# Attention's output projection and the final projection in blocks of seven products, at the head of the feed-forward's sequence

## The chip, the core and the metric

One core of a Trainium2 chip runs the whole kernel. The metric is device time in microseconds (us). TensorE (PE) multiplies matrices out of SBUF into PSUM, VectorE (DVE) and ScalarE (ACT) work on elements, GpSimd (POOL) does a few small things, and SyncE (SP) issues nearly all DMAs. Each engine works off its own list of instructions in order; semaphores make one wait for another.

## The reference, cut to what matters

A block of an encoder on 256 tokens of width 2048: a retention branch and a latent attention branch, merged by gates, then a feed-forward of width 8192. The stretch that the change is about:

```python
def _mixer(...):
    ...
    y_mla = my.reshape(B, S, MLA_V_W) @ w_mla_o                 # 256x2048 @ 2048x2048
    merged = jax.nn.sigmoid(g_ret) * y_ret + jax.nn.sigmoid(g_mla) * y_mla
    return merged @ w_out                                        # 256x2048 @ 2048x2048

def reference(...):
    ...
        h = h + _mixer(...)
        z = _rmsnorm(h, norm_mlp_g[l]) @ w_up[l]                 # 2048x8192
        h = h + jnp.square(jax.nn.relu(z)) @ w_down[l]           # 8192x2048
    return _rmsnorm(h, norm_f_g)
```

All inputs are float32.

## The kernel before, in words

**Products of two halves.** Every float32 operand is split into a rounded part `hi` and the remainder `lo`; a product is three matmuls (hi x hi, hi x lo, lo x hi). For weights the split is one cast on ACT (`hi`) and one subtraction on DVE (`lo`) of a tile of 128x1024, in `weights` (lines L168 and L169) or in `split` (L550 and L551). `hi` and `lo` lie in rings of buffers (4, in some stages 7), the raw weights in a ring of five.

**Eight and seven products.** Most large products are cut into blocks: two 128-row pieces of the inner dimension, two halves of the tokens (t), two column pieces of 512 (c). Done plainly (`Eight`), a block is eight products, 24 matmuls, in two parts of one weight tile each. Done by a Strassen-like scheme (`Seven`), it is seven products, 21 matmuls, in four parts. `Seven` needs sums of weights (`forms`, three DVE operations, L307, L316 and L317), splits of three 128x1024 tiles and one 128x512 tile, and sums of tokens (`combine`, L231 to L241 and a split), which one set serves for all columns. Its results pile up in four additional PSUM banks, and `partial` turns these into four corrections (`rest`) at the end of a half, a half being 1024 columns. The table `SEVEN` says at which places of the eight blocks of a half the sevens stand.

**What sets the order.** In the stages written with parts, `stream` lays out the order by hand (`manual_schedule`): at step n it issues the loads up to part n+6, the splits (`prep`) up to part n+4, the matmuls of part n, then what `after(n)` and the list `later` (steps to wait, work) hold for this step. Elsewhere a scheduler orders instructions.

**Around the change.** The attention's output projection (`mo`, `w_mla_o`) and the final projection (`wo`, `w_out`) are plain: `n_unit` walks over four column quarters of 512, each with two PSUM tiles (one per token half) and 16 inner pieces; L214, L215 and L217 are its three matmuls. Both are 384 matmuls. The first quarters of `mo` are interleaved with the last four attention heads. As a quarter of `mo` ends, `merge` multiplies it by its gate `gm` and adds `m1`, `merge_turn` transposes the result and splits it into `mg`, the final projection's tokens. As a quarter of `wo` ends, DVE adds it to the residual `hn` (L1220) and ACT sums its squares (L1221); `mlp_turn` transposes `hn` and cuts it into `hT` (L553, L554), the feed-forward's tokens, and `hc.make` forms their combinations. Then the feed-forward's `stream` begins with three early units (`z`), each in two halves, the first halves first; the second halves need all of `hT`. Steps of seven products (`zs`) and further units follow, and last the down projection (`dn`), of whose 64 blocks 22 are sevens.

Of the kernel before, what the change touches and what calls it, by code (L numbers as in the profile page):

```python
# [12 lines left out]
F32 = mybir.dt.float32  # L13
F32R = mybir.dt.float32r
# [5 lines left out]
P = 128  # L20
S = 256
# [20 lines left out]
KP = KT // 2  # L42
XC = 2, 10
EARLIES = 7, 15, 60
SEVEN = {"rv": ((2, 4, 5), (2, 4, 5)), "gr": ((3, 5), (2, 4, 5)), "yr": ((2, 4, 5), (2, 4, 5)), "gm": ((3, 5, 6), (2, 4, 5))}
DS = (4, 7, 9, 12, 14, 17, 19, 22, 24, 27), (3, 5, 7, 9, 11, 13, 15, 17, 19, 21, 24, 27)
KEPT = 3
MORE = 3
# [57 lines left out]
def block_kernel(ctx: ExitStack, tc: tile.TileContext, A):  # L106
# [233 lines left out]

    class Banks:
        def __init__(self, name, half, pairs, steps):
            self.name, self.half, self.q = name, half, {}
# [15 lines left out]
            PE.matmul(q, al, wh, start=False, stop=self.left[f] == 0)  # L359

    class Tokens:
        def __init__(self, pair, j, sets):
            self.pair, self.j, self.sets = pair, j, sets

        def load(self):
            pass
# [7 lines left out]
        def get(self, f):  # L374
            if f in Combos.RAW:
                return self.block(*Combos.RAW[f])
            c = self.sets[:, self.j]
            return c[:, 0, Combos.FORM[f]], c[:, 1, Combos.FORM[f]]

    class Eight:  # L380
# [528 lines left out]
    with ExitStack() as mctx:  # L909
# [159 lines left out]

        cq, ckv = Lora(cc[:, :LT]), Lora(cc[:, LT:])  # L1070
        mg = Pair("mg")
        mo = {}

        def mla_projections(g):
            j0 = 2 * (g % 2)
# [44 lines left out]
            SC.copy(v1, pss[1])  # L1120
            heads[g, "v"] = vs, v1

        def mo_part(c, kp):
            src = A["w_mla_o"][4 * c + kp // 2][:, kp % 2 * 2 : kp % 2 * 2 + 2]
            n_unit(mo[c], src, my, 2 * kp, 2, kp == 0, kp == 7)

        def mla_out_begin():
            for c in range(2):
                mo[c] = [mmps(f"mo{c}{t}") for t in range(2)]
            for kps in (range(4), range(4, 6)):  # L1130
                for c in range(2):
                    for kp in kps:
                        mo_part(c, kp)
                        yield

        SLOTS = (
            ((0, 2, 4, 6), (4, 6, 8, 10), (6, 8, 10, 12)),
# [23 lines left out]
        def merge(c):  # L1161
            cs = slice(c * 512, (c + 1) * 512)
            for t, ps in enumerate(mo[c]):
                V.tensor_tensor(out=gm[:, t, cs], in0=ps, in1=gm[:, t, cs], op=ALU.mult)
                V.tensor_tensor(out=gm[:, t, cs], in0=gm[:, t, cs], in1=m1[:, t, cs], op=ALU.add)

        def merge_turn(c):
            for jj in range(2):
                pT = atps(f"mt{c}{jj}")
                for j in range(2):  # L1170
                    for t in range(2):
                        o = j * S + t * P
                        k = 4 * c + 2 * jj + j
                        PE.transpose(pT[:, o : o + P], gm[:, t, k * P : (k + 1) * P], ident)
                split(*mg.span(4 * c + 2 * jj, 2), pT.rearrange("p (j n) -> p j n", j=2))

        for c in range(2):
            for kp in (6, 7):
                mo_part(c, kp)
            merge(c)  # L1180
        for c in range(2, 4):
            mo[c] = n_cols("mo", A["w_mla_o"], my, c, [None, lambda: merge_turn(c - 2), lambda: merge_turn(c - 1)][: c])
            merge(c)
        for c in (2, 3):
            merge_turn(c)

    rctx.close()
    hn = big("hn", shape=(P, 2, D))
    nc.sync.dma_start(hn, A["x"].rearrange("(t p) d -> p t d", p=P))
    hT = Pair("hT")  # L1190

    def mlp_turn(c):
        for jj in range(2):
            pT = atps(f"ht{c}{jj}")
            for j in range(2):
                kt = 4 * c + 2 * jj + j
                for t in range(2):
                    o = j * S + t * P
                    PE.transpose(pT[:, o : o + P], hn[:, t, kt * P : (kt + 1) * P], ident)
            for j in range(2):  # L1200
                kt = 4 * c + 2 * jj + j
                g = vec[:, V_MLP + kt : V_MLP + kt + 1]
                split(hT.hi(kt), hT.lo(kt), pT[:, j * S : (j + 1) * S], scale=g)
    zp = ctx.enter_context(tc.tile_pool(name="zp", bufs=1))
    hidd = ctx.enter_context(tc.tile_pool(name="hidd", bufs=1, space=bass.MemoryType.DRAM))
    hc = Combos("hc", hT)
    ssh = cp.tile([P, 2, 4], F32, name="ssh")
    rh2 = cp.tile([P, 2], F32, name="rh2")
    for c in range(4):
        cs = slice(c * 512, (c + 1) * 512)  # L1210
        pss = [mmps(f"wo{c}{t}") for t in range(2)]
        for kq in range(4):
            n_unit(pss, A["w_out"][4 * c + kq], mg, 4 * kq, 4, kq == 0, kq == 3)
            if kq == 0 and c:
                mlp_turn(c - 1)
        if c in (1, 2):
            for _ in hc.make(c - 1):
                pass
        for t in range(2):
            V.tensor_tensor(out=hn[:, t, cs], in0=pss[t], in1=hn[:, t, cs], op=ALU.add)  # L1220
            SC.activation(pss[t], hn[:, t, cs], AF.Square, accum_out=ssh[:, t, c : c + 1])  # L1221
    for t in range(2):
        V.reduce_sum(rh2[:, t : t + 1], ssh[:, t], axis=mybir.AxisListType.X)
    V.tensor_scalar(rh2, rh2, 1.0 / D, EPS, op0=ALU.mult, op1=ALU.add)
    V.reciprocal(rh2, rh2)

    hid = [hidd.tile([P, 2, S], F32, name=f"hid{i}") for i in range(FT // 2)]
    forms = big("forms", shape=(P, 4, 2, 512))

    def store(pair, n, t):  # L1230
        SC.activation(t, t, AF.Square)
# [7 lines left out]
    class Unit:  # L1239
# [11 lines left out]

        def mm(self, part):
            if part == 0:
                self.ps = atps(f"z{self.i}")
# [49 lines left out]
        return fn  # L1304

    early = [Unit(i, 0) for i in range(EARLY)]
    parts = [(e, h) for h in range(2) for e in early]
    units = list(range(EARLY, FT - ST - LATE))
    slots = [(u, j, h) for u in range(SU) for j in range(SJ) for h in (1, 3)][:-1]
    whole = [t for t in slots if t[2] == 3]  # L1310
# [17 lines left out]
        un = Unit(i, 0, drain(((0, 1), (1, 2))[n]))  # L1328
        parts += [(un, 0), (un, 1)]

    hp = ctx.enter_context(tc.tile_pool(name="hp", bufs=1))
    combs, sets = {}, {}
    ssf = cp.tile([P, 2, SSF], F32, name="ssf")
    rf = cp.tile([P, 2], F32, name="rf")
# [124 lines left out]
    making = iter(())  # L1459

    def after(n):
        nonlocal making, zo, keep, hn2, gt
        if n == 0:
            mlp_turn(3)
# [3 lines left out]
        elif n in MAKE:  # L1468
            making = hc.make(2 + MAKE.index(n))
        if n < 2 * EARLY or n % 2 == 0:  # L1470
            next(making, None)
        if hooks.get(n) == 0:
            hn2 = big("hn2", shape=(P, 2, D))
            G.dma_start(hn2, keep)
            gt = big("gt", shape=(P, 2, D))
            G.dma_start(gt[:, 0], A["norm_f_g"].partition_broadcast(P))
        elif hooks.get(n) == 1:
            for t in range(2):
                for c in range(2):
                    def one(t=t, c=c):  # L1480
                        later.append([1, finish(0, t, c, c)])

                    later.append([2 * t + c, one])
                    later.append([6 + 2 * t + c, lambda t=t, c=c: scale(t, c)])

    zo = keep = hn2 = gt = None
    rings(zp, MORE, True, forms)
    with tc.manual_schedule(engines=MANUAL):
        stream(parts, after)
        assert not later  # L1490
# [100 lines left out]
```

## Time and profile before

| | |
|---|---|
| median of 3 runs | 1566.04 us (1565.64 to 1566.29) |
| the profiled execution | 1566.54 us, of which 1564.8 from the first to the last instruction |
| busy: PE, DVE, ACT | 1551.3, 1316.0, 962.6 us |
| matmuls of `mo`, first and last start | 685.3 and 786.4 us |
| matmuls of `wo`, first and last start | 787.4 and 877.9 us |
| first matmul of the early units, of `zs` | 878.2 and 895.8 us |

A row of a timeline is start, duration, engine, line, operation, output <- inputs by the program's names, the shape, and in brackets the idle time of the engine before it and what ended that. A row of groups ends with busy time and mean duration in ns, then the engine's idle time before these instructions. A row of a stretch gives its length, the busy time of PE, weight loads, DVE, ACT and POOL, the granted TensorE clock (1.00 is full), the DMA's share and GB/s. Matmuls are drawn longer than the distance between their starts, since they overlap.

### The profile page before, as it was taken

The numbers are of one execution on the slowest core, as the hardware profiler recorded it, in microseconds if no ns is written. First come the engines' busy times: TensorE is split into PE (matmuls) and PEld (weight loads), VectorE is DVE, ScalarE is ACT, GpSimd is POOL, SyncE is SP. The second block draws the span as 40 slices with busy tenths as digits, with TensorE's granted clock in tenths as the row PEclk, the third lists the DMA queues.
The fourth block names the chain that finished last, engine by engine and source line by source line (L and its number), as shares of the span: only waits on it lengthen the run. The fifth ranks groups of instructions, "written<-read, shape, count | busy, mean of one in ns | idle before, by whom it ended". The sixth has DMA issues, their size and how long they took to land.

```text
span 1564.8 us, 21391 instructions
## 1 busy us (share of the span) xinstructions
PE 1551.3 (99%) x7655; PEld 1311.0 (84%) x7655; DVE 1316.0 (84%) x1787; ACT 962.6 (62%) x1416; POOL 39.3 (3%) x76
## 2 busy tenths in 40 slices
PE   9999999999999999999999999999999999999997
PEld 7888888888898888888888888888888888888886
DVE  7898877799976988976567689887978899989996
ACT  6645655566545667875445567676767766656664
POOL 0000000000000000000000000000000100000000
PEclk9999999999999999999999999999999999999999
DMA  9666755566656654444556657666675977686873
GB/s 319 207 203 208 230 164 161 159 201 206 206 168 220 213 197 143 157 136 161 185 206 211 236 196 247 214 226 232 207 249 188 376 265 245 237 304 211 266 255 115
DMA packets 107626, 333.70 MB, mean 213 GB/s; under 512 B 11264, under 2 KB 12160, under 8 KB 106496
## 3 DMA queue, kind: packets, MB, share of 16 engines
q1 hardware_dynamic: 104208, 318.71, 61.1%
q0 software_dynamic: 3168, 11.54, 1.9%
q10 hardware_dynamic: 144, 2.10, 0.4%
q8 instruction: 60, 0.98, 0.3%
q14 instruction: 46, 0.38, 0.1%
HBM read 319.72 MB, written 12.58 MB: 212 GB/s over the span
## 4 chain that ended last, share of the span: by engine, by line
PE 79%; DVE 1%; issue 1%; ACT 1%; DVEq 0%; POOLq 0%; POOL 0%; ACTq 0%
PE z L176 9%; PE dn L358 7%; PE dn L359 7%; PE dn L357 7%; PE z L180 5%; PE zs L333 2%; PE zs L334 2%; PE zs L335 2%; PE mo L214 2%; PE mo L215 2%; PE mo L217 2%; PE wo L214 2%; PE wo L215 2%; PE wo L217 2%; PE gm L357 2%; PE yr L358 2%
## 5 line engine op out<-in xcount | busy, mean ns | idle before, releaser
L551 DVE TENSOR_TENSOR lo<-raw,hi 128x1024 fp32r<-128x1024 f32 (+3 forms) x214 | 232.0, 1101 | 22.7 <-ACT hi L550 22.2
L169 DVE TENSOR_TENSOR lo<-raw,hi 128x1024 fp32r<-128x1024 f32 (+1 forms) x148 | 173.2, 1171 | 89.7 <-ACT hi L168 89.6
L168 ACT CAST hi<-raw 128x1024 fp32r<-128x1024 f32 (+1 forms) x148 | 149.6, 1011 | 155.9 <-PE mo L215 44.9
L550 ACT CAST hi<-raw 128x1024 fp32r<-128x1024 f32 (+3 forms) x214 | 200.0, 953 | 55.3 <-issue 9.5
L551 DVE TENSOR_TENSOR morelo<-raw,morehi 128x1024 fp32r<-128x1024 f32 (+1 forms) x118 | 127.1, 1098 | 18.8 <-ACT morehi L550 18.3
L550 ACT CAST morehi<-raw 128x1024 fp32r<-128x1024 f32 (+1 forms) x118 | 109.1, 949 | 10.5 <-issue 3.2
L550 ACT CAST hi<-forms 128x1024 fp32r<-128x1024 f32 x70 | 73.7, 1052 | 51.2 <-DVE forms L307 28.1
L176 PE MATMUL z<-hT,morehi 128*128 128x512 f32 x408 | 101.6, 391 | 0.0
L357 PE MATMUL dn<-hi,dd 128*128 128x512 f32 x230 | 89.6, 389 | 0.0
L359 PE MATMUL dn<-hi,dd 128*128 128x512 f32 x230 | 89.5, 389 | 0.0
L358 PE MATMUL dn<-lo,dd 128*128 128x512 f32 x230 | 89.5, 389 | 0.0
L551 DVE TENSOR_TENSOR lo<-forms,hi 128x1024 fp32r<-128x1024 f32 x70 | 85.0, 1221 | 5.3 <-ACT hi L550 4.9
L176 PEld LDWEIGHTS z<-hT,morehi 128*128 128x128 f32 x408 | 74.9, 188 | 14.4
L1266 ACT COPY hs<-z 128x512 f32<-128x512 f32 x40 | 23.5, 587 | 71.2 <-PE z L180 71.1
L357 PE MATMUL dn<-morehi,dd 128*128 128x512 f32 x156 | 60.7, 389 | 0.0
L358 PE MATMUL dn<-morelo,dd 128*128 128x512 f32 x156 | 60.7, 389 | 0.0
L359 PE MATMUL dn<-morehi,dd 128*128 128x512 f32 x156 | 60.7, 389 | 0.0
L180 PEld LDWEIGHTS z<-hT,morelo 128*128 128x128 f32 x408 | 55.6, 190 | 4.0
L176 PE MATMUL z<-hT,hi 128*128 128x512 f32 x232 | 57.9, 392 | 0.0
L180 PE MATMUL z<-hT,morelo 128*128 128x256 f32 x408 | 56.9, 282 | 0.0
L307 DVE TENSOR_TENSOR forms<-raw,sraw 128x1024 f32<-128x1024 f32 x46 | 56.1, 1219 | 0.3 <-DMA raw<-w_up_s 0.3
L358 PEld LDWEIGHTS dn<-lo,dd 128*128 128x128 f32 x230 | 43.2, 188 | 9.0
(500 smaller groups left out, 4193.9 us busy)
## 6 DMA issues: line engine op xcount, KB each, us to landing
raw<-w_down SPq DMA_DIRECT2D x106, 512.0 KB, 6.0
raw<-w_up SPq DMA_DIRECT2D x80, 512.0 KB, 5.1
raw<-w_rv SPq DMA_DIRECT2D x32, 512.0 KB, 4.8
raw<-w_rg SPq DMA_DIRECT2D x32, 512.0 KB, 4.3
raw<-w_gret SPq DMA_DIRECT2D x32, 512.0 KB, 4.4
raw<-w_ret_o SPq DMA_DIRECT2D x32, 512.0 KB, 5.0
raw<-w_gmla SPq DMA_DIRECT2D x32, 512.0 KB, 4.3
raw<-w_mla_o SPq DMA_DIRECT2D x32, 512.0 KB, 3.7
```

Of the source, the lines that this page charges most:

```text
L168: SC.copy(hi, raw)
L169: V.tensor_tensor(out=lo, in0=raw, in1=hi.bitcast(F32), op=ALU.subtract)
L176: PE.matmul(out, w[0][:, k], x.both(k0 + k), start=start and k == 0, stop=False)
L180: PE.matmul(out[:, :S], w[1][:, k], x.hi(k0 + k), start=False, stop=stop and k == n - 1)
L214: PE.matmul(out, x.hi(k0 + k, ts), w[0][:, k], start=start and k == 0, stop=False)
L215: PE.matmul(out, x.lo(k0 + k, ts), w[0][:, k], start=False, stop=False)
L217: PE.matmul(out, x.hi(k0 + k, ts), w[1][:, k], start=False, stop=stop and k == nk - 1)
L357: PE.matmul(q, ah, wh, start=start, stop=False)
L358: PE.matmul(q, ah, wl, start=False, stop=False)
L359: PE.matmul(q, al, wh, start=False, stop=self.left[f] == 0)
L550: SC.copy(hi, val)
L551: V.tensor_tensor(out=lo, in0=val, in1=hi.bitcast(F32), op=ALU.subtract)
```

## The change

Both projections are taken out of the scheduled part and become 68 parts of blocks at the head of the feed-forward's `stream` (the first six blocks of `mo`'s first half stay interleaved with the attention). `mo`'s second half has three sevens (blocks 0, 1, 2), `wo`'s first half two (4, 5) and its second three (4, 5, 6): eight of 32 blocks. The weights are laid out on the host in the order of the blocks. `merged`, `summed` and `begun` (the correction's addition ahead of the last block) take the place of the loops' ends; `plan` holds what happens after which part: transposes, combinations of tokens, the load of the residual. The early units become four, and the last transposes of `hn` follow the first three of their halves.

```diff
-EARLY, LATE = 3, 2
+EARLY, LATE = 4, 2
...
-MAKE = 7, 2 * EARLY + 18
+MAKE = 9, 2 * EARLY + 18
...
-SEVEN = {... "gm": ((3, 5, 6), (2, 4, 5))}
+SEVEN = {... "gm": ((3, 5, 6), (2, 4, 5)), "mo": ((), (4, 5, 6)), "wo": ((5, 6), (4, 5, 6))}
...
-        for c in range(2, 4):
-            mo[c] = n_cols("mo", A["w_mla_o"], my, c, [None, lambda: merge_turn(c - 2), lambda: merge_turn(c - 1)][: c])
-            merge(c)
-        for c in (2, 3):
-            merge_turn(c)
...
-    for c in range(4):
-        cs = slice(c * 512, (c + 1) * 512)
-        pss = [mmps(f"wo{c}{t}") for t in range(2)]
-        for kq in range(4):
-            n_unit(pss, A["w_out"][4 * c + kq], mg, 4 * kq, 4, kq == 0, kq == 3)
-            if kq == 0 and c:
-                mlp_turn(c - 1)
-        if c in (1, 2):
-            for _ in hc.make(c - 1):
-                pass
...
+    def merged(banks, t, c):
+        ...
+        if banks.rest:
+            r = banks.rest[t, c]
+            V.tensor_tensor(out=r, in0=p, in1=r, op=ALU.add)
+            p = r
+        V.tensor_tensor(out=g, in0=p, in1=g, op=ALU.mult)
+        V.tensor_tensor(out=g, in0=g, in1=m1[:, t, cs], op=ALU.add)
+
+    def summed(banks, t, c):
+        n = 2 * banks.half + c
+        h = hn[:, t, n * 512 : (n + 1) * 512]
+        V.tensor_tensor(out=h, in0=banks.q[ROLE[t, c]], in1=h, op=ALU.add)
+        SC.activation(banks.rest[t, c], h, AF.Square, accum_out=ssh[:, t, n : n + 1])
+
+    def begun(banks, t, c):
+        o = (2 * banks.half + c) * 512
+        h = hn[:, t, o : o + 512]
+        V.tensor_tensor(out=h, in0=banks.rest[t, c], in1=h, op=ALU.add)
+
+    def half_of(banks, src, x, seq, sets, first, done, soonest, early=None):
+        ...
+        def end():
+            sums = partial(banks, wsums)
+            later.extend([d, lambda: next(sums)] for d in range(2))
+            if early:
+                later.extend([1 + (t == 0), lambda t=t, c=c: early(banks, t, c)] for t in (1, 0) for c in range(2))
+
+        def over(part):
+            if part:
+                for c in range(2):
+                    for t in range(2):
+                        later.append([soonest[t, c], lambda t=t, c=c: done(banks, t, c)])
+        ...
+    slow = {(0, 0): 0, (1, 0): 1, (0, 1): 2, (1, 1): 3}
+    fast = {(0, 0): 0, (1, 0): 0, (0, 1): 1, (1, 1): 1}
+    half_of(mob[0], A["w_mla_o"], my, E8(6, 7), None, 0, merged, slow)
+    at(0, lambda: make(my, 0, wsets[0][:, :2]))
+    at(3, lambda: make(my, 2, wsets[0][:, 2:]))
+    base = len(parts)
+    half_of(mob[1], A["w_mla_o"], my, E8(3, 4, 5, 6) + S7(0, 1, 2) + E8(7), wsets[0], 0, merged, slow)
+    for i in range(4):
+        at(base + 3 + i, lambda i=i: merge_turn(i // 2, i % 2, mmps))
+    ...
+    half_of(wob[0], A["w_out"], mg, E8(0, 1, 2, 3, 7) + S7(4, 5) + E8(6), wsets[1], 4, summed, slow, begun)
+    at(base + 1, lambda: nc.sync.dma_start(hn, A["x"].rearrange("(t p) d -> p t d", p=P)))
+    for i in range(4):
+        at(base + 3 + i, lambda i=i: merge_turn(2 + i // 2, i % 2, atps))
+    at(base + 6, lambda: make(mg, 4, wsets[1][:, :2]))
+    at(base + 11, lambda: make(mg, 6, wsets[1][:, 2:]))
+    base = len(parts)
+    half_of(wob[1], A["w_out"], mg, E8(0, 1, 2, 3) + S7(4, 5, 6) + E8(7), wsets[1], 4, summed, fast, begun)
+    ...
+    for i in range(4):
+        at(base + 3 + i, lambda i=i: turned(i // 2, i % 2, mmps, 1))
+    at(base + 8, lambda: makings.append(hc.make(0)))
+    at(base + 14, lambda: makings.append(hc.make(1)))
+    off = len(parts)
+    for n, i in enumerate((0, 1, 2, 2)):
+        at(off + i, lambda n=n: turned(2 + n // 2, n % 2, atps, 0))
```

How the order moves, at three places. The first is ScalarE where a piece of the final projection is added to the residual: `hi` are casts of weights, the ACTIVATE with `ssh` is the sum of squares of `hn`. Before, at the end of the first quarter:

```order
L168 CAST hi_7606<-raw_7605 128x1024
L168 CAST hi_7624<-raw_7623 128x1024
L1221 ACTIVATE wo_7399,ssh<-hn 128x512
L1221 ACTIVATE wo_7400,ssh<-hn 128x512
L168 CAST hi_7642<-raw_7641 128x1024
L168 CAST hi_7660<-raw_7659 128x1024
```

Now, at the end of the first half:

```order
L550 CAST hi_7834<-raw_7797 128x1024
L1218 ACTIVATE wsums,ssh<-hn 128x512
L550 CAST hi_7856<-raw_7810 128x1024
L1218 ACTIVATE wsums,ssh<-hn 128x512
L550 CAST hi_7880<-raw_7832 128x1024
L1218 ACTIVATE wsums,ssh<-hn 128x512
```

The squares stood in pairs, and now stand singly, each ahead of one cast. The second place is VectorE at the same ends, where `lo` is the split that follows the cast `hi` of the same row. Before, at the end of the second quarter:

```order
L169 TENSOR_TENSOR lo_7785<-raw_7783,hi_7784 128x1024
L1220 TENSOR_TENSOR hn<-wo_7549,hn 128x512
L1220 TENSOR_TENSOR hn<-wo_7550,hn 128x512
L169 TENSOR_TENSOR lo_7803<-raw_7801,hi_7802 128x1024
L169 TENSOR_TENSOR lo_7821<-raw_7819,hi_7820 128x1024
```

Now, at the end of the first half, behind the additions of the corrections (`wsums`):

```order
L1223 TENSOR_TENSOR hn<-wsums,hn 128x512 x2
L551 TENSOR_TENSOR lo_7835<-raw_7797,hi_7834 128x1024
L1223 TENSOR_TENSOR hn<-wsums,hn 128x512 x2
L1217 TENSOR_TENSOR hn<-wo_7480,hn 128x512
L551 TENSOR_TENSOR lo_7857<-raw_7810,hi_7856 128x1024
L1217 TENSOR_TENSOR hn<-wo_7488,hn 128x512
L551 TENSOR_TENSOR lo_7881<-raw_7832,hi_7880 128x1024
```

Four additions alternate with four splits, where two stood together, and four more additions stand ahead. The third place is TensorE at the step from the final projection to the feed-forward; `ht` are transposes of `hn`. Before:

```order
L217 MATMUL wo_7905<-lo_8052,mg_5247 128x512 x2
L176 MATMUL z_8138<-hT_7390,hi_8126 128x512 x8
L180 MATMUL z_8138<-hT_7390,lo_8127 128x256 x8
L1199 MATMUL ht_8155<-con,hn 128x128 x4
L1199 MATMUL ht_8164<-con,hn 128x128 x4
L176 MATMUL z_8194<-hT_7390,hi_8130 128x512 x8
```

Now:

```order
L359 MATMUL wo_7872<-morehi_67_8166,mg_5247 128x512
L176 MATMUL z_8260<-hT_6939,morehi_68_8180 128x512 x8
L180 MATMUL z_8260<-hT_6939,morelo_68_8181 128x256 x8
L1169 MATMUL ht_8277<-con,hn 128x128 x4
L176 MATMUL z_8296<-hT_6939,morehi_69_8192 128x512 x8
L180 MATMUL z_8296<-hT_6939,morelo_69_8193 128x256 x8
L1169 MATMUL ht_8313<-con,hn 128x128 x4
```

The transposes behind the first early half are now those of the third quarter of `hn`, and the fourth quarter's come two halves later.

More of the change, by code (lines that the diff above doesn't have):

```diff
@@ L361, in block_kernel, with __init__ @@
     class Tokens:
-        def __init__(self, pair, j, sets):
-            self.pair, self.j, self.sets = pair, j, sets
+        def __init__(self, pair, j, sets, first=0):
+            self.pair, self.j, self.sets, self.first = pair, j, sets, first
         def load(self):
@@ L1121, in mla_projections @@
             heads[g, "v"] = vs, v1
-        def mo_part(c, kp):
-            src = A["w_mla_o"][4 * c + kp // 2][:, kp % 2 * 2 : kp % 2 * 2 + 2]
-            n_unit(mo[c], src, my, 2 * kp, 2, kp == 0, kp == 7)
+        mob = [Banks("mo", half, KP, len(at)) for half, at in enumerate(SEVEN["mo"])]
         def mla_out_begin():
[L1128 to L1134, printed above, removed]
+            rings(None, 0, False, None)
+            for j in range(6):
+                d = Eight(mob[0], A["w_mla_o"][0, j], Tokens(my, j, None))
+                for part in range(2):
+                    d.load(part)
+                    d.prep(part)
+                    d.mm(part)
+                    yield
         SLOTS = (
@@ new lines, in summed @@
+    def summed(banks, t, c):
[4 more added lines that the diff above has]
+    def begun(banks, t, c):
+        o = (2 * banks.half + c) * 512
+        h = hn[:, t, o : o + 512]
+        V.tensor_tensor(out=h, in0=banks.rest[t, c], in1=h, op=ALU.add)
+    steps = 0
+    def half_of(banks, src, x, seq, sets, first, done, soonest, early=None):
+        nonlocal steps
+        last = max((m for m, (k, j) in enumerate(seq) if k == 7), default=None)
+        def end():
[6 more added lines that the diff above has]
+                for c in range(2):
+                    for t in range(2):
+                        later.append([soonest[t, c], lambda t=t, c=c: done(banks, t, c)])
+        for m, (k, j) in enumerate(seq):
+            if k == 7:
+                st = Seven(banks, src[banks.half, j], Tokens(x, j, sets, first), steps, end if m == last else None)
+                parts.extend((st, h) for h in range(4))
+                steps += 1
+            else:
+                st = Eight(banks, src[banks.half, j], Tokens(x, j, None))
+                parts.extend((st, h) for h in range(2))
+        st.after = over
@@ L1306, in block_kernel @@
     early = [Unit(i, 0) for i in range(EARLY)]
-    parts = [(e, h) for h in range(2) for e in early]
+    parts += [(e, h) for h in range(2) for e in early]
     units = list(range(EARLY, FT - ST - LATE))
```

112 lines of the change are left out of this document (60 added, 52 removed).

## The prediction

> **What bounds the kernel now.** I read the page's busy times first, then the stretches in which the two projections run, then the groups inside one of them.
>
> ```profile
> PE 1551.3 (99%) x7655; PEld 1311.0 (84%) x7655; DVE 1316.0 (84%) x1787; ACT 962.6 (62%) x1416; POOL 39.3 (3%) x76
> ...
> 729.50:787.40 57.90, 57.90 (x274) 48.28 (x272) 36.84 (x41) 24.83 (x28) 0.00 (x0) 1.00 0.61 203
> 787.40:878.20 90.80, 90.80 (x420) 75.46 (x418) 59.10 (x69) 45.17 (x62) 0.00 (x0) 1.00 0.60 200
> 878.20:895.80 17.60, 17.60 (x106) 15.59 (x105) 13.31 (x21) 11.07 (x17) 0.00 (x0) 1.00 0.72 263
> 1300.00:1400.00 100.00, 100.00 (x443) 82.81 (x442) 96.71 (x121) 62.60 (x80) 0.00 (x0) 1.00 0.76 265
> ...
> L169 DVE TENSOR_TENSOR lo<-raw,hi 128x1024 fp32r<-128x1024 f32 x29 | 35.5, 1224 | 25.5 <-ACT hi L168 25.5
> L168 ACT CAST hi<-raw 128x1024 fp32r<-128x1024 f32 x28 | 29.5, 1053 | 34.8 <-PE wo L215 32.7 <-ACT wo L1221 1.3 <-ACT hc L550 0.7
> ```
>
> The columns of a stretch are length, then busy time of PE, weight loads, DVE, ACT and POOL, granted clock, DMA. In the first three rows (output projection after its first 144 matmuls, final projection, head of the feed-forward) TensorE has no idle time and VectorE is 64 to 76% busy. The two group rows are the final projection's: ScalarE waits 32.7 us for TensorE to give buffers back, and VectorE only for ScalarE. So TensorE bounds this stretch, and its time falls with its instructions for as long as VectorE follows.
>
> **What TensorE gains.** Eight blocks issue 21 matmuls where they issued 24: 24 fewer. The old loop also turned the third column quarter of the merged rows twice (40 transposes in all, 32 now): 8 fewer.
>
> ```profile
> 1550.16 0.39 PE L357 MATMUL dn<-over,dd 128*128 128x512 f32 x1
> ...
> 1552.43 0.39 PE L358 MATMUL dn<-over,dd 128*128 128x512 f32 x1
> ...
> 860.50 0.62 PE L217 MATMUL wo<-lo,mg 128*128 128x512 f32 x2
> 860.96 1.03 PE L1199 MATMUL ht<-con,hn 128*128 128x128 f32 x8
> 861.75 0.48 PE L214 MATMUL wo<-hi,mg 128*128 128x512 f32 x1
> 862.06 0.40 PE L215 MATMUL wo<-hi,mg 128*128 128x512 f32 x1
> ```
>
> A matmul is drawn 0.39 us long, but starts count: ten lie between the first two rows, 2.27 us, so 0.227 each. Eight transposes take 0.79, and the matmul behind them 0.31 where 0.227 is usual: 0.88 in all, 0.44 per four. Gain: 24 x 0.227 + 0.88 = 6.3 us. Loads change in shape, not in bytes, and the planned count of DMAs is the same, so I cost them at nothing except below.
>
> **What VectorE pays.** A block of eight products needs two splits of 128x1024; one of seven needs three and a half, plus the sums of weights. Both stand in the last stage's timeline (start, duration):
>
> ```profile
> 1250.17 1.22 DVE L307 TENSOR_TENSOR forms<-raw,sraw 128x1024 f32<-128x1024 f32 x1
> 1251.31 0.69 DVE L551 TENSOR_TENSOR comb<-dq,comb 128x512 fp32r<-128x512 f32 x1
> 1251.91 1.22 DVE L551 TENSOR_TENSOR lo<-sraw,hi 128x1024 fp32r<-128x1024 f32 x1
> 1253.05 0.68 DVE L316 TENSOR_TENSOR forms<-forms,sraw 128x512 f32<-128x512 f32 x1
> 1253.76 0.69 DVE L317 TENSOR_TENSOR forms<-forms,raw 128x512 f32<-128x512 f32 x1
> 1254.37 2.50 DVE L551 TENSOR_TENSOR morelo<-forms,morehi 128x1024 fp32r<-128x1024 f32 x2
> 1256.79 0.69 DVE L551 TENSOR_TENSOR morelo<-raw,morehi 128x512 fp32r<-128x512 f32 x1
> 1257.39 0.69 DVE L551 TENSOR_TENSOR dd<-hl,dd 128x512 fp32r<-128x512 f32 x1
> 1257.99 2.36 DVE L551 TENSOR_TENSOR lo<-raw,hi 128x1024 fp32r<-128x1024 f32 x2
> 1260.27 0.42 DVE L1356 TENSOR_TENSOR dq<-hl 128x256 f32<-128x256 f32 x1
> 1260.72 0.29 DVE L1359 TENSOR_TENSOR dq<-dq,hl 128x128 f32<-128x128 f32 x1
> 1261.05 0.29 DVE L1360 TENSOR_TENSOR dq<-dq,hl 128x128 f32<-128x128 f32 x1
> ...
> 818.67 0.88 DVE L554 SCALAR_TENSOR_TENSOR hT<-ht,vec,hT 128x256 fp32r<-128x256 f32 x2
> ```
>
> From start to start a seven costs 7.22 less the 0.60 of the tokens' split (comb) among it: 6.6 us, against 21 x 0.227 = 4.8 on TensorE. Two 1024-wide splits cost 2.28 (1.14 each), against 24 x 0.227 = 5.4. A 512-wide operation costs 0.60, and 0.72 when the next one reads its result; a 256-wide one 0.34 to 0.45, a 128-wide one 0.2 to 0.33, a pair of scaled ones 0.8. Each seven thus puts VectorE 1.8 us behind, each eight lets it catch up 3.1, and the merges, sums and turns between them fall on VectorE besides.
>
> I compare the two engines from the moment at which they meet: the end of the output projection's first half, which VectorE must await before it merges (its splits are then four parts ahead, and there they stop). The end point is where TensorE must await VectorE: the transposes behind the first early feed-forward part read the sum hn of the third quarter.
> - TensorE: 183 + 186 + 183 matmuls x 0.227 = 125.2, twelve groups of four transposes x 0.44 = 5.3, one half unit of the feed-forward 2.8 (six of them and eight transposes fill the 17.6 us of the third stretch above). Sum 133.3.
> - VectorE: 32 splits for eights and early units x 1.14 = 36.5; eight sevens x 6.6 = 53; merges of both halves 5.3 + 8.2; three rounds of bank sums 7.9; 14 additions into hn x 0.60 = 8.4; eight splits of turned rows x 0.60 = 4.8; four cuts of hT x 0.8 = 3.2; combinations of tokens 16 (three blocks' at 3.9, three smaller ones). Sum 143.
>
> TensorE therefore loses 143 - 133.3 = 9.7 us however the work is strewn, unless these rows cost less there. By the time that the first merge is due VectorE has idled for lack of anything further that it may do, so no earlier lead helps.
>
> **What queues add.** In the new order ScalarE's squares stand right behind VectorE's additions and ahead of the next cast (`summed`, `slow`): the split after an addition waits for addition, square and cast in turn.
>
> ```profile
> 855.71 0.69 DVE L1220 TENSOR_TENSOR hn<-wo,hn 128x512 f32<-128x512 f32 x1 [0.22 <-PE wo L217]
> 856.26 0.59 ACT L1221 ACTIVATE wo<-hn 128x512 f32<-128x512 f32 x1
> 856.38 1.22 DVE L169 TENSOR_TENSOR lo<-raw,hi 128x1024 fp32r<-128x1024 f32 x1
> 856.78 0.19 ACT L1221 ACTIVATION_READ_ACCUMULATOR wo<-hn 128x1 f32 x1
> 856.88 0.58 ACT L1221 ACTIVATE wo<-hn 128x512 f32<-128x512 f32 x1
> ...
> raw<-w_out SPq DMA_DIRECT2D x32, 512.0 KB, 3.8
> ```
>
> Before, the split at 856.38 starts in the midst of the square, since its cast was done ahead. Now: 0.69 + square with accumulator 0.62 (856.26 to 856.88) + cast 1.05 + hand-overs 0.1 = 2.46 instead of 0.60, four times: 7.4 us of VectorE's idle time. Bounds: 0, if TensorE and not VectorE ends the stretch, and 7.4; I take 7.4 because VectorE is behind there by then. Behind the second half's additions the same pair of squares delays only cuts that have TensorE's next parts as cover. The last operands of three token combinations wait some 0.6 us each for ScalarE's cast behind them; two are exposed: 1.3. A combination holds two of five raw buffers, so the load of a final-projection block that follows it is issued 3.4 us of VectorE's work before its split, and takes 3.8 to land and 1.05 to be cast: 1.6 (bounds 0 and 4). The two-megabyte load of hn stands on SP's queue ahead of eight parts of loads; they have over 10 us until use: nothing.
>
> Sum: 9.7 + 7.4 + 1.3 + 1.6 = 20.0 lost, 6.3 gained, +13.7. Against the profiled execution's 1566.5 this gives 1580.2; the median before, 1566.0, lies 0.5 lower: 1580.
>
> [...]
>
> **Rivals.**
> - VectorE keeps up. For it: at 1300 to 1400 VectorE is busy 96.7% and TensorE still never idles, with a third of the blocks in seven products. Against: those blocks carry no merges and turns. It decides from the point at which VectorE's 143 falls under 133: 1566.0 - 6.3 = 1560. Chance 0.10.
> - Only the surplus counts, the queues' waits falling where TensorE is behind anyway: 9.7 - 6.3 = +3.4, with 0 to 4 for loads 1567 to 1574. For it: ScalarE is busy only half of the time, and the casts may run further ahead. Chance 0.24.
> - The clock falls in the wait ahead of the transposes. From the split of the last block, VectorE has 12 us of work to the sum and TensorE 6.3: a gap of near 6 us.
>
> ```profile
> 1554.00:1556.00 2.00, 1.76 (x8) 1.13 (x6) 0.25 (x2) 0.46 (x1) 0.00 (x0) 1.00 0.99 372
> 1558.00:1560.00 2.00, 0.00 (x0) 0.00 (x0) 1.33 (x3) 1.32 (x2) 0.55 (x1) 0.90 0.00 0
> 1560.00:1562.00 2.00, 0.00 (x0) 0.00 (x0) 0.10 (x1) 0.01 (x1) 0.00 (x0) 0.50 0.89 328
> ...
> 1.19 3.59 PE L573 MATMUL spin<-cold 128*128 128x512 bf16 x8 [1.19 <-DVE cold L570]
> 4.26 2.93 PE L622 MATMUL first<-x,hi 128*128 128x512 f32 x6
> ```
>
> After the last matmul (before 1556) the granted clock, the seventh figure, halves by 1560. At the head eight 512-wide matmuls take 3.6 us, twice what they take later, so some 5 us at half rate cost 2.5: 1582.5. Chance 0.25. [...]
> - The forecast without it, 1575 to 1581: 0.33. Further stalls in the head of the feed-forward, where VectorE is busy 76%: over 1588, 0.08.
>
> **How the numbers follow.** The forecast is 1580. The range 1567 to 1588 leaves out the first rival and the worst case, 0.18. About 0.2% (3.1 us) is what a measurement tells from no change: faster 0.10; same 0.06, from the low end of the second rival; slower 0.84. The forecast's own range, with the clock's fall or without, is 1574 to 1586.
>
> **What would show it.** After: no idle TensorE up to the merges, then waits on splits in the second half of the final projection, the longest ahead of the transposes of hn; VectorE above 95% busy there, or idle on ScalarE's casts four times by 1.9 us; 32 fewer TensorE instructions. I am wrong if TensorE stays full through the stretch (the sum of VectorE was too high), or if its waits lie elsewhere, on DMA or PSUM banks.

## The result and the profile after

The changed kernel takes 1589.24 us (median of 4 runs, 1588.11 to 1589.48) against 1566.1 before: a ratio of 1.0148, 95% interval 1.0134 to 1.0162. That is 23.1 us slower. The forecast was 13.7 slower, and its range ended 1.2 us below the measured time.

The stretches of the changed kernel, in the columns of the prediction's first fence (length, then busy time of PE, weight loads, DVE, ACT, POOL, then granted clock, DMA, GB/s):

```profile
728.00:800.00 72.00, 72.00 (x331) 59.60 (x330) 68.11 (x85) 38.98 (x44) 0.00 (x0) 1.00 0.64 226
800.00:850.00 50.00, 47.77 (x219) 38.70 (x218) 40.20 (x52) 23.40 (x32) 0.00 (x0) 1.00 0.47 158
850.00:900.00 50.00, 34.75 (x126) 25.56 (x125) 44.50 (x58) 23.11 (x33) 0.00 (x0) 0.83 0.43 144
900.00:960.00 60.00, 59.47 (x315) 50.96 (x316) 47.94 (x64) 40.60 (x65) 3.97 (x7) 0.97 0.64 217
```

The loss lies between 800 and 915 us. Ahead of it TensorE is full and VectorE 95% busy; in the third row TensorE is busy for 35 of 50 us and the granted clock is 0.83. What TensorE waited for from 650 to 960 us (total, times, longest), and below it what VectorE waited for from 738 to 900 us:

```profile
PE wo L357 <- DVE hT L554: 6.3, 4, 2.2
PE ht L1169 <- DVE hn L1217: 6.1, 2, 5.6
PE wo L358 <- DVE morelo L551: 2.1, 1, 2.1
PE wo L359 <- DVE mg L551: 1.7, 1, 1.7
...
DVE lo L551 <- ACT hi L550: 5.9, 5, 1.7
DVE morelo L551 <- ACT morehi L550: 5.8, 6, 1.8
DVE mg L551 <- ACT mg L550: 2.5, 2, 1.9
DVE hT L554 <- ACT hT L553: 2.2, 4, 0.5
```

Nearly all that TensorE waits for is VectorE: for PSUM banks that VectorE empties (hT, since the four additional banks of the second half's sevens are those in which `hn` was transposed), for splits (morelo, mg), and last for the sum of the third quarter of `hn`. VectorE in turn waits for ScalarE alone, whose casts await data of their own; behind 762 us these are loads and VectorE's results, and none of VectorE's waits leads back to TensorE. So the chain to follow is VectorE's.

From VectorE's rows between the first merge (738.65) and the end of the third quarter's additions (899.84), adding starts and gaps: 142.6 us of work (the forecast's term was 143), 17.4 us of waits, and 1.2 us of gaps under 0.07 us. The waits have four main sources. First the squares. VectorE's rows, and ScalarE's of the same moment:

```profile
836.29 0.68 DVE L1217 TENSOR_TENSOR hn<-wo,hn 128x512 f32<-128x512 f32 x1
838.70 1.23 DVE L551 TENSOR_TENSOR lo<-raw,hi 128x1024 fp32r<-128x1024 f32 x1 [1.73 <-ACT hi L550]
...
837.00 0.63 ACT L1218 ACTIVATE wsums<-hn 128x512 f32<-128x512 f32 x1 [5.45 <-DVE hn L1217]
837.54 0.19 ACT L1218 ACTIVATION_READ_ACCUMULATOR wsums<-hn 128x1 f32 x1
837.63 1.04 ACT L550 CAST hi<-raw 128x1024 fp32r<-128x1024 f32 x1
```

Addition, square, cast, split, one after the other, four times: 1.73 to 1.79 us of idle VectorE each, 7.0 in all. Second, the cuts of the transposed `hn`, which come in pairs from one PSUM bank:

```profile
854.17 0.47 DVE L554 SCALAR_TENSOR_TENSOR hT<-ht,vec,hT 128x256 fp32r<-128x256 f32 x1
855.19 0.48 DVE L554 SCALAR_TENSOR_TENSOR hT<-ht,vec,hT 128x256 fp32r<-128x256 f32 x1 [0.54 <-ACT hT L553]
856.12 1.23 DVE L551 TENSOR_TENSOR morelo<-wforms,morehi 128x1024 fp32r<-128x1024 f32 x1 [0.45 <-ACT morehi L550]
...
850.25 0.46 ACT L553 ACTIVATE hT<-ht,vec 128x256 fp32r<-128x256 f32 x1
854.68 0.47 ACT L553 ACTIVATE hT<-ht,vec 128x256 fp32r<-128x256 f32 x1 [3.97 <-DVE hT L554]
```

ScalarE's second cast (854.68) waits for VectorE's first cut (854.17 to 854.64), and VectorE's second cut waits for that cast. Behind two of the four banks the weight's split (as at 856.12) waits for the cast behind it as well: 4 x 0.54 and 2 x 0.45, 3.1 us. The rows show this order; what forces it was not tried. In the kernel before, such cuts came from two banks: ScalarE casts one half of each, VectorE cuts these, and ScalarE's second pair starts (818.16) as VectorE's first cut ends (0.47 after 817.65).

```profile
816.38 0.84 ACT L553 ACTIVATE hT<-ht,vec 128x256 fp32r<-128x256 f32 x2
817.65 0.87 DVE L554 SCALAR_TENSOR_TENSOR hT<-ht,vec,hT 128x256 fp32r<-128x256 f32 x2
818.16 0.87 ACT L553 ACTIVATE hT<-ht,vec 128x256 fp32r<-128x256 f32 x2 [0.94 <-DVE hT L554]
```

Third, loads that were held up by a combination's raw buffers: 2.1 us at 824 to 830, and 1.4 at 890, where the load is one of the feed-forward (with the combinations made later, in a run below, this wait is gone):

```profile
889.01 1.05 ACT L550 CAST morehi<-raw 128x1024 fp32r<-128x1024 f32 x1 [1.70 <-DMA raw<-w_up]
890.09 1.23 DVE L551 TENSOR_TENSOR morelo<-raw,morehi 128x1024 fp32r<-128x1024 f32 x1 [1.45 <-ACT morehi L550]
```

Fourth, 2.5 us ahead of splits of the merged rows, at 758 and 762. There ScalarE's casts wait for TensorE's transposes (in the groups, `mg` on ScalarE: 10.4 us idle, all for the transposes), so VectorE is still ahead of TensorE then:

```profile
L551 DVE TENSOR_TENSOR mg<-mt,mg 128x512 fp32r<-128x512 f32 x8 | 5.5, 685 | 2.5 <-ACT mg L550 2.5
L550 ACT CAST mg<-mt 128x512 fp32r<-128x512 f32 x8 | 4.7, 586 | 10.4 <-PE mt L1185 10.4
```

The rest is 1.0 at two combinations and 0.2 at one split. The same stretch seen from TensorE, where it meets the chain:

```profile
892.55 1.11 PE L180 MATMUL z<-hT,morelo 128*128 128x256 f32 x8
899.30 1.50 PE L1169 MATMUL ht<-con,hn 128*128 128x128 f32 x4 [5.65 <-DVE hn L1217]
900.45 3.56 PE L176 MATMUL z<-hT,morehi 128*128 128x512 f32 x8
903.85 1.12 PE L180 MATMUL z<-hT,morelo 128*128 128x256 f32 x8
904.81 0.60 PE L1169 MATMUL ht<-con,hn 128*128 128x128 f32 x4
...
914.40 0.50 PE L176 MATMUL z<-hT,hi 128*128 128x512 f32 x1 [0.53 <-DVE hT L554]
```

Adding up how far TensorE's starts lie apart beyond what each kind takes back to back (0.227 us for 512 columns, 0.12 for 256, 0.11 for 128), TensorE loses 26.1 us from the end of the output projection's first half to the transposes at 899.30, and 3.4 more up to 960 us than the kernel before does there. Less the 6.3 gained, that is 23.2. Elsewhere the two profiled executions differ by 0.5.

### The profile page after: what moved, and what is told of

It is laid out like the page before. It is cut to its first block, busy times and chain, and to the rows that moved or that the text cites. A ratio compares the mean times of both kernels' runs of the same rounds, so it can differ in the third digit from the quotient of the medians.

```text
span 1587.5 us, 21429 instructions
## 1 busy us (share of the span) xinstructions
PE 1556.2 (98%) x7623; PEld 1310.0 (83%) x7623; DVE 1373.0 (86%) x1873; ACT 979.2 (62%) x1440; POOL 39.2 (2%) x76
## 4 chain that ended last, share of the span: by engine, by line
PE 70%; DVE 6%; ACT 2%; issue 2%; DMA 1%; DVEq 0%; POOLq 0%; POOL 0%; ACTq 0%
PE z L176 9%; PE dn L358 7%; PE dn L359 7%; PE dn L357 7%; PE z L180 5%; PE zs L333 2%; PE zs L334 2%; PE zs L335 2%; PE gm L359 2%; PE gm L357 2%; PE yr L357 2%; PE yr L358 2%; PE yr L359 2%; PE gm L358 2%; PE gr L357 2%
## 5 line engine op out<-in xcount | busy, mean ns | idle before, releaser
L551 DVE TENSOR_TENSOR lo<-raw,hi 128x1024 fp32r<-128x1024 f32 (+3 forms) x256 | 275.8, 1089 | 47.9 <-ACT hi L550 45.9
L550 ACT CAST hi<-raw 128x1024 fp32r<-128x1024 f32 (+3 forms) x256 | 238.2, 943 | 77.1 <-PE mo L359 13.2
L551 DVE TENSOR_TENSOR morelo<-raw,morehi 128x1024 fp32r<-128x1024 f32 (+1 forms) x132 | 147.5, 1139 | 18.2 <-ACT morehi L550 17.5
L550 ACT CAST morehi<-raw 128x1024 fp32r<-128x1024 f32 (+1 forms) x132 | 126.3, 982 | 19.4 <-DMA raw<-w_out 8.7
L168 ACT CAST hi<-raw 128x1024 fp32r<-128x1024 f32 (+1 forms) x84 | 82.2, 980 | 76.4 <-issue 19.2
L169 DVE TENSOR_TENSOR lo<-raw,hi 128x1024 fp32r<-128x1024 f32 (+1 forms) x84 | 94.8, 1130 | 28.9 <-ACT hi L168 28.9
L357 PE MATMUL dn<-hi,dd 128*128 128x512 f32 x196 | 76.2, 389 | 0.0
L358 PE MATMUL dn<-lo,dd 128*128 128x512 f32 x196 | 76.2, 389 | 0.0
L359 PE MATMUL dn<-hi,dd 128*128 128x512 f32 x196 | 76.2, 389 | 0.0
L357 PE MATMUL dn<-morehi,dd 128*128 128x512 f32 x190 | 74.0, 390 | 0.0
L359 PE MATMUL dn<-morehi,dd 128*128 128x512 f32 x190 | 73.9, 389 | 0.0
L176 PEld LDWEIGHTS z<-hT,hi 128*128 128x128 f32 x272 | 50.0, 188 | 11.1 <-DVE hT L554 1.4
```

The costliest lines, as they stand in the source:

```text
L168: SC.copy(hi, raw)
L169: V.tensor_tensor(out=lo, in0=raw, in1=hi.bitcast(F32), op=ALU.subtract)
L176: PE.matmul(out, w[0][:, k], x.both(k0 + k), start=start and k == 0, stop=False)
L357: PE.matmul(q, ah, wh, start=start, stop=False)
L358: PE.matmul(q, ah, wl, start=False, stop=False)
L550: SC.copy(hi, val)
```

## The experiments

Two theories were put against each other. A: VectorE's chain, its work plus its own waits, sets the end, and what TensorE waits ahead of the chain's end is absorbed. B: TensorE's waits add up, each where it stands.

### The squares a step later

```diff
-        SC.activation(banks.rest[t, c], h, AF.Square, accum_out=ssh[:, t, n : n + 1])
+        later.append([0, lambda: SC.activation(banks.rest[t, c], h, AF.Square, accum_out=ssh[:, t, n : n + 1])])
```

> Edit: the square of each piece of hn is issued one step later, behind the next cast; nothing is left out. Theory A (VectorE's chain sets the end: its work of 142.6 us from the first merge to the sum of the third quarter of hn, plus its own waits; what TensorE waits ahead of that is absorbed): the four waits of 1.73 us for cast behind square go, so 6.9 us less, 1582.3. Theory B (each wait of TensorE adds by itself): in that place TensorE waits only 0.8 us ahead of its transposes, so 1588.4, and the waits for banks, splits and the last sum stay as they are.

1580.96 us, ratio to the kernel before 1.0096 (1.0081 to 1.0111): 8.3 less than the changed kernel. VectorE's row of the same addition and split:

```profile
836.13 0.68 DVE L1217 TENSOR_TENSOR hn<-wo,hn 128x512 f32<-128x512 f32 x1
836.73 1.22 DVE L551 TENSOR_TENSOR lo<-raw,hi 128x1024 fp32r<-128x1024 f32 x1
```

The split follows without a wait, and the transposes of the third quarter start at 892.16 instead of 899.30, 7.1 earlier. The rest, 1.2, comes from behind them. Theory A is out by 1.3 us and B by 7.4; the forecast's 7.4 for the squares holds.

### Work added where TensorE waits

```diff
-        for j in range(2):
+        for j in list(range(2)) * (4 if c < 2 else 1):
             kt = 4 * c + 2 * jj + j
             for t in range(2):
                 o = j * S + t * P
                 PE.transpose(pT[:, o : o + P], hn[:, t, kt * P : (kt + 1) * P], ident)
```

> Edit: the transposes of the first two quarters of hn are done four times over, the same values into the same bank: 48 more, 48 x 0.11 = 5.3 us more work for TensorE in the final projection's second half. Theory A: VectorE's chain sets the end and does not wait for these, so the time stays at 1589 within 1 us, and the wait of 5.7 us ahead of the last transposes of hn shrinks instead. Theory B: TensorE's work and waits add up: 1594.5.

1589.65 us, ratio 1.0152 (1.0137 to 1.0167): 5.3 us more work for TensorE moves the time by 0.4. A had expected the wait ahead of the last transposes to shrink. It did not; those for banks did, from 6.3 to 2.5, and the granted clock from 850 to 900 us rose from 0.83 to 0.94:

```profile
PE ht L1169 <- DVE hn L1217: 6.1, 2, 5.7
PE wo L358 <- DVE lo L551: 2.7, 2, 1.8
PE wo L357 <- DVE hT L554: 2.5, 2, 1.3
...
850.00:900.00 50.00, 35.53 (x160) 26.92 (x158) 44.61 (x58) 22.92 (x31) 0.00 (x0) 0.94 0.42 143
```

So 5.3 us of work fits ahead of the chain's end. It did not only fill waits: by the author's estimate from TensorE's starts, half rate costs some 8 us in the changed kernel and 4 here, so theory B, with the clock's gain counted in, would be out by about 1 us and not by 5, and this run alone hardly tells the two apart. That the 6.3 us of waits for banks cost nothing by themselves rests on VectorE's list, which waits for nothing of TensorE there, and on the other runs.

### No sevens, and sevens in the output projection alone

```diff
-"mo": ((), (4, 5, 6)), "wo": ((5, 6), (4, 5, 6))
+"mo": ((), ()), "wo": ((), ())
...
-E8(3, 4, 5, 6) + S7(0, 1, 2) + E8(7)
+E8(3, 4, 5, 6, 0, 1, 2, 7)
-E8(0, 1, 2, 3, 7) + S7(4, 5) + E8(6)
+E8(0, 1, 2, 3, 7, 4, 5, 6)
-E8(0, 1, 2, 3) + S7(4, 5, 6) + E8(7)
+E8(0, 1, 2, 3, 4, 5, 6, 7)
```

The tokens' combinations for these blocks go too; in the second kernel those of the output projection and its three sevens stay.

> Edit: all 32 blocks of both projections as eights, the rest of the new order kept (halves of 1024, squares one by one, four early units). Theory A: VectorE has some 95 us of work against 139 of TensorE, TensorE bounds, and only the eight doubled transposes are gained: 1566.0 - 0.9 = 1565.2, no wait of TensorE in the stretch. Rival (the new order itself costs: its queues, banks and loads): 1570 or more.

> Edit: the three sevens of the output projection kept, the final projection's five made eights. Theory A: VectorE falls behind in the output projection by 3 x 1.8 us and the tokens' sums, and catches up 3.1 us in each of the final projection's eights before TensorE must wait: nine matmuls less than without sevens, 1565.2 - 2.0 = 1563.1. Rival (what falls behind is never made up, the merges alone make TensorE wait): 1566 to 1572.

1567.86 us (ratio 1.0014, 1.0005 to 1.0023) and 1566.82 (1.0005, 0.9995 to 1.0014). Both expectations of A were missed, by 2.7 and 3.7 us. TensorE waits nowhere in the projections, but both kernels wait in the second early halves, for cuts of the last quarter of `hn`:

```profile
PE z L176 <- DVE hT L554: 1.2, 3, 0.5
```

With the restart behind each, starts lie 2.0 to 2.4 us further apart there than back to back. Without sevens the clock also fell for a few matmuls behind them in the profiled execution (1569.19 us): 0.43 us apart, some 1.3 us more. Of the second kernel's 3.7 some 1 us stays unexplained. So the new order has a cost of its own of 2 to 3 us with three sevens and with none. The rows point to the fourth quarter's cuts, two in one bank, which stand too close to the halves that need them; a run below tests this.

### The two cuts of a bank a step apart

```diff
-        later.append([d, mlp_turn(c, jj, ps)])
+        cut = mlp_turn(c, jj, ps)
+        later.extend([d + (j if c < 2 else 0), lambda j=j: cut(j)] for j in range(2))
```

(`mlp_turn`'s `cut` takes `j` as an argument instead of looping over it.)

> Edit: in the final projection's second half the two cuts of a bank of turned hn stand a step apart instead of back to back; nothing is left out. Theory A (VectorE's chain, waits and work, sets the end): its four waits of 0.54 us for ScalarE's second cast of a bank and the two of 0.45 behind them go, 3.1 us: 1586.1. Theory B (TensorE's own waits add up): the banks come free a step later, so the waits for them grow by up to 4 x 1 us: 1589 to 1593.

1585.83 us, ratio 1.0127 (1.0112 to 1.0142): 3.4 less. The six waits are gone from VectorE's rows, and the transposes of the third quarter start at 895.24, 4.1 earlier, while TensorE's longest wait for a bank grew from 2.2 to 4.0. A again.

### TensorE kept busy in the gap

```diff
+    def fill():
+        early[1].ps = mmps("z1")
+        for _ in range(48):
+            PE.transpose(early[1].ps[:, :P], hn[:, 0, :P], ident)
+
+    at(off, fill)
```

> Edit: 48 transposes of a finished piece, into a bank that is overwritten later, stand ahead of the transposes that wait for the sum of the third quarter of hn: 48 x 0.11 = 5.2 us of the 5.9 us gap. If TensorE's half rate behind the gap (eight matmuls 0.43 us apart instead of 0.227) is the price of idling, they come 0.227 apart and 1.6 us are gained: 1587.6. If the rate is set by something else, the same rows stay at 0.43 and the time at 1589.

1592.08 us, ratio 1.0164 (1.0149 to 1.0179): neither number.

```profile
895.08 5.40 PE L1290 MATMUL z<-con,hn 128*128 128x128 f32 x48
900.87 0.33 PE L1169 MATMUL ht<-con,hn 128*128 128x128 f32 x1 [0.39 <-DVE hn L1217]
901.46 0.55 PE L1169 MATMUL ht<-con,hn 128*128 128x128 f32 x3 [0.27 <-DVE hn L1217]
901.77 2.10 PE L176 MATMUL z<-hT,morehi 128*128 128x512 f32 x8
...
904.66 0.60 PE L1169 MATMUL ht<-con,hn 128*128 128x128 f32 x4
...
915.98 0.50 PE L176 MATMUL z<-hT,hi 128*128 128x512 f32 x1 [0.52 <-DVE hT L554]
```

The mechanism is as expected: eight matmuls take 2.10 instead of 3.56 us, and from the first transposes to the next 3.8 us pass instead of 5.5. But nothing is gained. From the first transposes to the last wait for a cut 15.1 us pass, as in the changed kernel (899.30 to 914.40): behind the gap, too, VectorE and ScalarE set the pace. Half rate cost no time here. Why this kernel is slower by 2.9 is only partly seen: in the profiled execution (1590.82 us, the fastest of four) the transposes start 1.6 later, 0.7 of it already before the edit's place, 0.9 in a later load of the feed-forward's weights. The other 1.3 is open.

### The feed-forward's combinations later

```diff
-    at(base + 8, lambda: makings.append(hc.make(0)))
-    at(base + 14, lambda: makings.append(hc.make(1)))
     off = len(parts)
+    at(off + 2, lambda: makings.append(hc.make(0)))
+    at(off + 6, lambda: makings.append(hc.make(1)))
```

> Edit: the first two combinations of the feed-forward's tokens are made behind the first early units instead of in the final projection's second half; the same work, later. Theory A: VectorE's chain to the sum of the third quarter loses 2 x 3.9 us of work and 0.5 to 2 us of waits, and VectorE has room behind it (75 to 85% busy): 8 to 10 us less, 1579 to 1581. If the room behind is too small, the gain is given back there in waits ahead of the steps with seven products: down to 4 us less, 1585. Theory B (work as such does not matter, only the order of queues and banks): 1589.

1583.01 us, ratio 1.0109 (1.0092 to 1.0126): 6.2 less, between A's two cases. The transposes of the third quarter start at 889.72, 9.6 earlier, so VectorE's work does count as such: to that point its rows hold 134.9 us of work instead of 142.6. Some 3 us are given back, about half of it in the wait for cuts in the second early halves, which grows from 0.5 to 1.9.

```profile
PE ht L1169 <- DVE hn L1217: 3.5, 3, 2.6
PE z L176 <- DVE hT L554: 1.9, 3, 0.8
```

### Two banks cut by turns

On the kernel with sevens in the output projection alone:

```diff
-    for n, i in enumerate((0, 1, 2, 2)):
-        at(off + i, lambda n=n: turned(2 + n // 2, n % 2, atps, 0))
+    def quarter(c):
+        cuts = [mlp_turn(c, jj, atps) for jj in range(2)]
+        later.extend([0, lambda cut=cut, j=j: cut(j)] for j in range(2) for cut in cuts)
+
+    for c in (2, 3):
+        at(off + c - 2, lambda c=c: quarter(c))
```

> Edit: the kernel with sevens in the output projection alone, and the last two quarters of hn turned two banks at a time, behind the first and the second early half unit, their cuts taken by turns from the two banks. Theory: TensorE's three waits of 0.8 us in the second early halves go, and nothing waits from the output projection to the feed-forward: 1566.8 - 2.4 = 1564.4, 1.6 us faster than the kernel before. Rival (VectorE is late there by its work, not by the two casts of one bank waiting for each other): 1566.8.

1563.39 us, ratio 0.9983 (0.9974 to 0.9993), 3.4 less than without this edit and faster than the kernel before. TensorE has no wait left from 700 to 960 us. So the cost found above lay in these cuts. The edit changes two things at once, how the banks take turns and how late the cuts stand, and does not tell them apart.

### Eight, five and five sevens

The first kernel has all eight sevens with the four edits above together that took time away (squares, cuts a step apart, combinations, two banks by turns), and blocks 6 and 7 exchanged in the final projection's first half; the second the same without the sevens of its second half, and with the feed-forward's combinations where the change put them; the third only turns those three sevens into eights.

```diff
-E8(0, 1, 2, 3, 7) + S7(4, 5) + E8(6)
+E8(0, 1, 2, 3, 6) + S7(4, 5) + E8(7)
```

> Edit: all eight sevens stay; the squares a step later, the cuts of the second and third stretch by turns as in the runs before, the two combinations of the feed-forward's tokens behind the first early units, and blocks 6 and 7 exchanged in the final projection's first half (the last turned piece of the merged rows is then needed two parts later). Theory A: VectorE's work to the sum of the third quarter of hn is 142.6 - 7.8 = 134.8, its remaining waits 4 to 5 (2.5 ahead of the merged rows' splits, 0.5, 1.5 to 2 for loads), against 133.3 of TensorE: 6 us lost, 1566 - 6.3 + 6 = 1566 to 1567. Rival (the sevens' cost lay in the waits alone): TensorE bounds, 1560. Rival (the gains of the single edits simply add): 1589.2 - 8.3 - 3.4 - 6.2 - 3.4 = 1567.9.

> Edit: the sevens of the output projection and of the final projection's first half kept (five), its second half in eights; squares later, cuts by turns, blocks 6 and 7 exchanged; the feed-forward's combinations stay where they are. Theory A: VectorE's work to the sum of the third quarter falls to about 122 against 135 of TensorE, which bounds again: six matmuls less than with three sevens, 1563.4 - 1.4 = 1562.0. Rival (the lag behind the output projection's merges still holds TensorE up by 1.5 to 2 us): 1563.5 to 1564.

> Edit: only the last three sevens (the final projection's second half) made eights, everything else as changed. Theory A: VectorE's work to the sum falls by 3 x 4.3 and one combination, about 16 to 20 us, TensorE's rises by 2.0; the waits of the squares fall where VectorE is no longer late. Of the 26 us lost 2 to 6 stay, and behind the sum some 3: 1567 to 1571. Rival (the late stretch is bound by banks and queues, the blocks' kind does not matter): 1585 or more.

1567.40 us (ratio 1.0008, 0.9999 to 1.0017), 1562.18 (0.9973, 0.9963 to 0.9984) and 1569.74 (1.0022, 1.0013 to 1.0032). All three as A had it, within half a microsecond of its range. The first also fits the sum of the single gains (1567.9), so it tells A from "the waits were all" (1560), not from that sum. Its remaining waits of TensorE, and then the stretches of the second:

```profile
PE wo L357 <- DVE hT L554: 2.5, 1, 2.5
PE ht L1169 <- DVE hn L1216: 2.1, 2, 1.9
```

```profile
728.00:800.00 72.00, 72.00 (x331) 59.60 (x330) 68.33 (x85) 38.89 (x44) 0.00 (x0) 1.00 0.65 227
800.00:890.00 90.00, 90.00 (x437) 75.50 (x436) 77.63 (x99) 51.47 (x75) 0.00 (x0) 1.00 0.62 203
890.00:960.00 70.00, 70.00 (x373) 60.46 (x372) 60.62 (x76) 47.44 (x68) 5.60 (x10) 1.00 0.63 216
```

With eight sevens and two thirds of VectorE's waits removed (5.7 us of 17.4 are left), VectorE still ends the stretch. With five, TensorE is full and 4.1 us are gained; 15 matmuls and eight transposes fewer are 15 x 0.227 + 0.88 = 4.3. Of the changed kernel's 23.1 us, turning its last three sevens into eights, with the combination that served one of them, takes away 19.5.

## Why the prediction was wrong

The direction and the mechanism were right, and so were most of the terms. The time was 9.2 us over the forecast and 1.2 over the range, because VectorE's chain has waits that no term named: 17.4 us in all, where "what queues add" had 10.3.

- **What TensorE gains**, 6.3: 32 instructions fewer in the page (7623 against 7655); the kernel with five sevens gains what its own share of this sum says.
- **What VectorE pays**, 143 against 133.3: measured 142.6. That the surplus counts however it is strewn was right as well: work added to TensorE ahead of the chain's end moved the time by 0.4, and taking 7.7 us of work and 2.0 of waits from VectorE moved the sum of the third quarter by 9.6.
- **What queues add**: squares 7.4, measured 7.0, and 8.3 with what follows; combinations' casts 1.3, measured 1.0; a held-up load 1.6, measured 2.1, with a second one, at the feed-forward's first weights, of 1.4 that was not counted.
- **The step that failed first** is the term "four cuts of hT x 0.8". As work this holds. But the row that it was read from showed two cuts back to back that came from two different banks. In the changed kernel both halves of one bank are cut in a row, and each pair costs 0.5 to 1.0 of waiting: 3.1 us, which went when the cuts were set a step apart.
- **The second** is the starting point. "By the time that the first merge is due VectorE has idled" was right, but it is not the last time that it idles for TensorE: the transposes of the merged rows hold it up 2.5 us, 20 us later. The two engines had to be compared from there on.
- **The third** is the sentence that the second half's squares delay "only cuts that have TensorE's next parts as cover": 3.4 us are lost behind the sum, where nothing was forecast. About 1.2 of them went with the squares. That the rest is again pairs of cuts from one bank is read from the rows (0.54 us of waiting at each of four banks) and not tested in this kernel.

The sums agree: 142.6 of work, 17.4 of waits and 1.2 of small gaps make 161.2 where the forecast had 143 + 10.3 = 153.3. VectorE started 1.2 before TensorE ended the half, and the first transposes need only the first of the last two additions (0.6), which leaves 6.1 more lost than the 20.0 forecast; 3.4 come behind.

Of the rivals, "VectorE keeps up" and "only the surplus counts" fell. The clock did fall, in three places instead of one (to 0.50 at 862.70, 876.35 and 896.83 us, 6.83 us each), and yet in the changed kernel the rival's price of 2.5 us was not paid: while TensorE runs at half rate VectorE's chain goes on, and TensorE only meets it with a shorter wait (from the first transposes to the last wait for a cut 15.1 us passed, with half rate or without). The waits for PSUM banks that the prediction named as a sign of error were there, 6.3 us, and were no cause.

## What to carry to other kernels

Where an engine off the critical path will fall behind, follow its own list from the last point at which it waited for the bound engine, and count every wait in it, not only its work; what the bound engine waits for on the way is then a symptom, and giving it more to do there cost next to nothing here (0.4 us for 5.3 of work). A duration that is read from a pair of rows holds for that pair's buffers only: see whether both came from one PSUM bank (here a pair from one bank waited 0.5 to 1.0 us). When a scheme trades the bound engine's work for another's, do it only in as many blocks as the other engine's slack pays for (here, of three, five and eight blocks out of 32, five was fastest; six and seven were not tried).

## What was not expected of the hardware

The granted clock fell without any long gap, where the rival had it fall in one of near 6 us. Between 853.84 and 864.14 us TensorE had four waits of 1.1 to 2.2 us with three to six matmuls between them; then twelve matmuls came 0.43 us apart, from 864.71 to 869.4.

```profile
855.87:859.29 3.42, 1.96 (x8) 1.33 (x9) 2.18 (x4) 2.11 (x5) 0.00 (x0) 1.00 0.62 231
859.29:862.70 3.41, 1.25 (x6) 0.61 (x4) 2.85 (x5) 1.63 (x4) 0.00 (x0) 1.00 0.00 0
862.70:866.11 3.41, 2.31 (x7) 1.61 (x6) 2.87 (x4) 2.30 (x3) 0.00 (x0) 0.50 0.47 154
866.11:869.53 3.42, 3.42 (x10) 2.65 (x9) 3.38 (x5) 1.72 (x3) 0.00 (x0) 0.50 0.00 0
869.53:872.94 3.41, 3.41 (x16) 2.66 (x15) 3.38 (x7) 0.44 (x1) 0.00 (x0) 1.00 0.00 0
```

In the changed kernel's trace the granted clock changes six times from 20 to 1535 us: it falls to 0.50 at 862.70, 876.35 and 896.83, and is full again at 869.53, 883.18 and 903.66. These times lie 6.82, 6.83 or 13.65 us apart, two or four times the 3.41 us of the rows above. Count each matmul with its distance from start to start (0.227, 0.12 and 0.11 us as above, twice that at half clock), not with the length that is drawn: TensorE is then in use for 0.47, 0.29, 0.57, 1.00 and 0.96 of the five stretches. With that whole time cut into such stretches, the clock fell behind three, with use of 0.02, 0.28 and 0.29, and behind none of the other 433 at full clock, of which the lowest has 0.47. It came back behind three at half clock, with 0.96 to 1.00, and not behind the three with 0.15, 0.57 and 0.73. In the kernel before, no stretch has a use under 0.54, and the clock stays full from 20 to 1535 us. The figures of use are estimates from the starts in these two traces.

Transposes counted as use as well: with 48 of them in a row (5.40 us, in the run with the gap filled) the granted clock stayed at 1.00 from 895 to 905 us, where the changed kernel shows 0.68 and 0.63 in the two halves of that time.
